# A two-layer hybrid decoder: seven block products for the output projection and most of the MLP's first matrix, with weight sums made by transfers

## The chip, the cores and the metric

The kernel runs on one core of a Trainium2 chip. The metric is the device time of one execution in microseconds; before the change it is 1337.68 us (median of three runs, 1336.81 to 1337.95). The engines are named as in the profile: PE is TensorE (PEld are its weight loads), DVE is VectorE, ACT is ScalarE, POOL is GpSimd, SP issues most transfers.

## What is computed

The reference is a decoder trunk with two layers over 512 tokens of width 1024, in float32. What matters here:

```python
def hybrid_layer(x, ...):
    h = rmsnorm(x, norm_mix)
    z = h @ w_in                                   # q, k, v | mLSTM q, k, v, o | gates
    ...                                            # att (512 wide), hm (512 wide)
    mixed = sigmoid(g_a) * (att @ w_att_branch) + sigmoid(g_m) * (hm @ w_m_branch)
    x = x + mixed @ w_out                          # 512x1024 @ 1024x1024
    u = relu(rmsnorm(x, norm_ffn) @ w_ff1)         # 512x1024 @ 1024x4096
    return x + (u * u) @ w_ff2                     # 512x4096 @ 4096x1024
```

`rmsnorm(x, g)` is `x * rsqrt(mean(x*x) + 1e-6) * g` with one factor per token.

## The kernel before

**Precision.** Each float32 operand of a large product is split into a high and a low piece of type float32r: ScalarE copies to the high one, VectorE subtracts it from the value to make the low one. `mm3` (line 207) then issues three matmuls into one PSUM bank, high x high, high x low, low x high. Weights come from HBM through SP's queue into raw tiles and are split on the way (`chunk`, line 164, in the mixer; `w_split`, line 820, in the MLP). Matmuls have a stationary operand of 128x128 and mostly 512 moving columns.

**Order of work.** Programs for the engines are written out as lists of steps. `weave` (line 251) runs a list `fill`, whose entries have a width, and inserts the steps of `side` at the places given. A planner at build time then fixes each engine's order: an instruction may go ahead of others whose operands are not ready, and what stands under `tc.high_priority()` (loads, splits, reads out of PSUM) goes first. Each engine runs its own list in order. A pool with n buffers makes the n+1st tile wait until the first one's readers are done.

**The mixer** (line 359) makes the projections, attention and mLSTM. At its end `ev_m` (line 786) multiplies the second branch with its gate and adds the first one, and splits the result tile by tile (`mixed`, 8 pairs of tiles of 128 features x 512 tokens). The output projection (lines 795 to 803) is `tok_steps` over these eight: two halves of 512 columns, 8 x 4 x 3 matmuls each; `ev_x` adds the result to the residual `xtok`.

**The norm** (`Norm`, line 275): `turn(k)` transposes 128 columns of the residual with four PE transposes, multiplies by the gain and splits (the tiles `i`); `squares` sums squares on ScalarE. The factor of the token isn't applied to the activations. In the MLP it was made with `columns` (one factor for each token), spread along the free axis with `along` (a diagonal, a float32 matmul with ones and a copy, line 310), and multiplied in `evac` (line 876), which reads a slot out of PSUM on VectorE: `max(ps, 0) * row`, then a square on ScalarE.

**The MLP** (line 806) goes through the 4096 hidden columns in four parts of 1024. A *first slot* (`First`, line 855) makes 256 hidden columns: 8 blocks of the contraction x 2 x 3 = 48 matmuls with the weights stationary and 512 tokens moving. The second matrix of a part (`slots_of`, line 921) is a 1024x1024 block with 512 tokens; it is computed as 2x2 blocks in seven products instead of eight (a Winograd form of Strassen's scheme). A product is 24 matmuls: left operand `a` of 256 tokens x 512 stationary, right operand of 512 x 512 moving. The sums and differences of weight blocks (`w_minus`) and of activation blocks (`u_op`) are made on VectorE; `gain` (line 845) adds a PSUM pair to the residual. While the second matrix of one part runs, the first slots of the next part stand between its products: p1, f, p5, p6, f, p3, p7, f, p2, f, p4. `prepare` (line 1011) writes the loads and splits of weights five half slots ahead.

## Time and profile before

| | before |
|---|---|
| median of the runs shown | 1337.68 us |
| span of the profiled execution | 1335.6 us |
| its own time (the span and some 2.1 us around it, taken from the median) | 1337.7 us |
| PE busy | 1312.4 us, 98% |
| DVE busy | 926.3 us, 69% |
| ACT busy | 666.4 us, 50% |
| POOL busy | 106.7 us, 8% |
| transfers | 125.02 MB, 30% of 16 engines' span |

A line of the profile's groups reads: source line, engine, operation, tile written <- tiles read, sizes, count | busy us, mean ns of one | idle time of the engine before them and what ended it. A line of the timeline reads: start, duration, engine, line, operation and tiles, count. Matmuls overlap, so the mean of one (about 390 ns) is a latency; the distance of starts is the price.

### The profile page before, as it was taken

What the parts mean: (1) busy time and instruction counts of PE and PEld (TensorE: products, weight loads), DVE (VectorE), ACT (ScalarE), POOL (GpSimd) and SP (SyncE); (2) the same over time, 40 slices, a digit from 0 to 9 for tenths busy, and PEclk for the clock granted to TensorE, in tenths of its full rate; (3) what the DMA queues carried; (4) which work ended last, traced back from release to release, by engine and by line L of the source; (5) the groups of instructions that cost most, each with busy time, mean ns of one, the idle gap of its engine ahead of it and who ended that gap; (6) DMA issues with size and microseconds to landing.
All of it is one profiled execution on the core that took longest, in us unless ns stands there. A gap on an engine that the chain in (4) does not pass through costs nothing.

```text
span 1335.6 us, 16885 instructions
## 1 busy us (share of the span) xinstructions
PE 1312.4 (98%) x6106; PEld 1078.1 (81%) x6106; DVE 926.3 (69%) x1409; ACT 666.4 (50%) x1201; POOL 106.7 (8%) x215
## 2 busy tenths in 40 slices
PE   8999999999999999999999999999999999999998
PEld 6877788888788888888888777888887888888886
DVE  4688764474576876868947887554646778678687
ACT  5458765544334344343554687554434444344343
POOL 4512310000000000000015013000000000000000
PEclk9999999999999999999999999999999999999999
DMA  5322122421523133131024221243216242322211
GB/s 151 108 72 72 56 79 74 140 95 64 189 95 126 63 127 125 64 119 46 34 65 123 67 71 64 72 122 96 99 54 207 73 132 81 125 95 95 95 48 63
DMA packets 87282, 125.02 MB, mean 94 GB/s; under 512 B 8216, under 2 KB 45184, under 8 KB 87200
## 3 DMA queue, kind: packets, MB, share of 16 engines
q1 hardware_dynamic: 86240, 123.30, 29.3%
q8 instruction: 48, 0.79, 0.2%
q10 hardware_dynamic: 576, 0.53, 0.1%
q0 software_dynamic: 384, 0.13, 0.1%
q14 instruction: 34, 0.28, 0.1%
HBM read 121.84 MB, written 2.10 MB: 93 GB/s over the span
## 4 chain that ended last, share of the span: by engine, by line
PE 88%; DVE 6%; ACT 4%; issue 1%; DMA 1%; POOL 0%; ACTq 0%; SPq 0%; DVEq 0%; POOLq 0%
PE mm L45 82%; PE aux L45 4%; PE aux L49 2%; ACT t L574 1%; DVE wl L191 1%; ACT wh L190 1%; DVE t L561 1%; DVE t L611 0%; DMA w<-in_w_in_dram 0%; DVE t L201 0%; ACT wh L825 0%; DVE t L538 0%; ACT junk L287 0%; DVE t L579 0%; DMA grow<-in_norm_mix_dram 0%
## 5 line engine op out<-in xcount | busy, mean ns | idle before, releaser
L45 PE MATMUL mm<-i,wh 128*128 128x512 f32 x1664 | 522.6, 393 | 2.1 <-DVE a L661 1.2
L45 PEld LDWEIGHTS mm<-i,wh 128*128 128x128 f32 x1664 | 307.7, 188 | 65.8 <-DVE a L661 2.0
L45 PE MATMUL mm<-i,wl 128*128 128x512 f32 x832 | 324.8, 390 | 0.0
L191 DVE TENSOR_TENSOR wl<-w,wh 128x512 fp32r<-128x512 f32 (+1 forms) x208 | 140.4, 677 | 131.7 <-ACT wh L190 126.8
L190 ACT ACTIVATE wh<-w 128x512 fp32r<-128x512 f32 (+1 forms) x208 | 127.2, 612 | 146.9 <-PE mm L45 123.8
L825 ACT ACTIVATE wh<-raw 128x1024 fp32r<-128x1024 f32 x112 | 118.3, 1056 | 151.9 <-PE mm L45 116.4
L45 PEld LDWEIGHTS mm<-i,wl 128*128 128x128 f32 x832 | 156.2, 188 | 33.0 <-issue 0.5
L45 PE MATMUL mm<-wh,uh 128*128 128x512 f32 x448 | 174.5, 389 | 0.0
L45 PE MATMUL mm<-wh,ul 128*128 128x512 f32 x448 | 174.3, 389 | 0.0
L45 PE MATMUL mm<-wl,uh 128*128 128x512 f32 x448 | 174.3, 389 | 0.0
L826 DVE TENSOR_TENSOR wl<-raw,wh 128x1024 fp32r<-128x1024 f32 x112 | 135.9, 1219 | 37.8 <-ACT wh L825 37.4
L45 PE MATMUL mm<-wh,i 128*128 128x512 f32 (+1 forms) x512 | 149.8, 371 | 0.4 <-ACT wh L190 0.4
L825 ACT ACTIVATE wh<-f 128x1024 fp32r<-128x1024 f32 x64 | 67.2, 1056 | 118.8 <-PE mm L45 92.3
L45 PEld LDWEIGHTS mm<-wh,i 128*128 128x128 f32 x512 | 92.7, 189 | 15.9 <-ACT wh L190 0.8
L826 DVE TENSOR_TENSOR wl<-f,wh 128x1024 fp32r<-128x1024 f32 x64 | 77.7, 1221 | 30.3 <-ACT wh L825 30.1
L45 PEld LDWEIGHTS mm<-wh,ul 128*128 128x128 f32 x448 | 84.1, 188 | 17.5
L45 PEld LDWEIGHTS mm<-wh,uh 128*128 128x128 f32 x448 | 84.1, 188 | 17.4
L45 PEld LDWEIGHTS mm<-wl,uh 128*128 128x128 f32 x448 | 84.1, 188 | 17.3
L45 PE MATMUL mm<-wl,i 128*128 128x512 f32 (+1 forms) x256 | 94.7, 370 | 0.0
L879 DVE SCALAR_TENSOR_TENSOR u<-mm,t 128x1024 f32<-128x1024 f32 x32 | 39.1, 1222 | 69.2 <-PE mm L45 69.1
L849 DVE TENSOR_TENSOR x<-x,mm 128x1024 f32<-128x1024 f32 x64 | 77.2, 1217 | 13.6 <-PE mm L45 13.6
L45 PE MATMUL mm<-wh,a 128*128 128x512 f32 x256 | 81.4, 393 | 0.0
(214 smaller groups left out, 1619.0 us busy)
## 6 DMA issues: line engine op xcount, KB each, us to landing
w<-in_w_in_dram SPq DMA_DIRECT2D x128, 256.0 KB, 2.6
f<-in_w_ff_dram SPq DMA_DIRECT2D x64, 512.0 KB, 3.7
raw<-in_w_ff_dram SPq DMA_DIRECT2D x64, 512.0 KB, 3.5
w<-in_w_out_dram SPq DMA_DIRECT2D x32, 256.0 KB, 2.5
w<-in_w_att_branch_dram SPq DMA_DIRECT2D x16, 256.0 KB, 2.5
w<-in_w_m_branch_dram SPq DMA_DIRECT2D x16, 256.0 KB, 2.5
w<-in_w_in_dram SPq DMA_DIRECT2D x16, 128.0 KB, 2.1
out_dram<-x SPq DMA_DIRECT2D x8, 256.0 KB, 2.2
```

Source lines behind the costliest of these rows:

```text
L45: return nc.tensor.matmul(*args, **kw)
L49: return nc.tensor.transpose(*args)
L190: sc.activation(wh[:, :off], raw[:, :off], AF.Copy)
L191: ve.tensor_tensor(wl[:, :off], raw[:, :off], f32(wh[:, :off]), op=ALU.subtract)
L561: ve.copy_predicated(dst, tri_i.unsqueeze(1).to_broadcast([P, 2, P]), p4[:, :, 1, :])
L574: sc.activation(s3[:, i, :], s3[:, i, :], AF.Exp, bias=m[:, i:i + 1], accum_out=den[:, i:i + 1])
L825: sc.activation(hi, r, AF.Copy)
L826: ve.tensor_tensor(lo, r, f32(hi), op=ALU.subtract)
L849: ve.tensor_tensor(xh, xh, ps, op=ALU.add)
L879: ve.scalar_tensor_tensor(dst, self.ps, 0.0, rowf[0].unsqueeze(1).to_broadcast([P, 2, T]), op0=ALU.max, op1=ALU.mult)
```

## The change

1. **Output projection.** `mixer` returns the unsplit sum as two tiles of 4 x 128 features x 512 tokens (`mixed`); the add is done on POOL. `mlp` begins with the projection, as one `second(None, mixed)`: seven block products in the order 1, 2, 5, 6, 3, 7, 4, in halves.
2. **First matrix.** The first 512 hidden columns stay as two plain slots (`Plain`, which reads out with `Relu` and `Square` on ScalarE). Each further group of 512 columns (`first`, seven groups in a layer) is done as seven block products of 24 matmuls, with the weight blocks stationary (512 x 256) and the left blocks moving (256 tokens). The combinations of the normed activations are made once a layer (`left_blocks`: 4 sums of high and low, 4 differences, 4 splits). Results are gathered in the tile `u`: `copy` on ScalarE, `finish` as a sum on VectorE and `Relu` and `Square` on ScalarE. Two groups stand between the products of each of the parts 0 to 2, by (2, 3, 3, 2, 2, 2, 0) after p1, p5, p6, p3, p7, p2, p4; the group of part 0 stands alone before them.
3. **Weight sums.** Signs are moved to the left operands and the gains, so that the right operands are plain sums. They are built by accumulating transfers (`accum_op=ALU.add`) on POOL's queue (`Weights`): b12+b11, then +b22, then +b21 in one tile, b22+b12 in the other.
4. **Norm factor.** relu(r h)^2 = r^2 relu(h)^2, so the MLP leaves the factor out and `gain` multiplies each result of the second matrix by r^2 = 1/v of its token (`inverse`), two half-width operations in place of one.
5. **Buffers.** Raw weights 9, splits 4 (`SPL`), which is also how many units ahead weights are prepared. A pool `half` for the whole kernel holds the attention's result, `mixed` and the hidden columns of the parts 1 and 3. `sel` and `cm2` are made in each layer.

The diff, cut to its core:

```diff
-            self.acts[k] = split(ps, self.gain(k), get=lambda: inp.tile([P, T], F32R, tag="i", name=nm("i")))
+            if self.big is None:
+                self.big = [inp.tile([P, KT, T], F32R, tag=f"i{n}", name=nm("i")) for n in range(2)]
+            to = [t[:, k, :] for t in self.big]
+            self.acts[k] = split(ps, self.gain(k), get=lambda: to.pop(0))
...
+        def inverse(self):
+            v = sm([P, NB], "nv")
+            ve.tensor_tensor(v, self.ss[:, :, 0], self.ss[:, :, 1], op=ALU.add)
+            ve.tensor_scalar(v, v, 1.0 / D, EPS, op0=ALU.mult, op1=ALU.add)
+            self.inv = sm([P, 2, NB], "ninv", 2)
+            ve.reciprocal(self.inv[:, 0, :], v)
+            ve.tensor_scalar(self.inv[:, 1, :], self.inv[:, 0, :], -1.0, None, op0=ALU.mult)
...
                 ve.tensor_tensor(sgm[g][m], sgm[g][m], ps, op=ALU.mult)
-                ve.tensor_tensor(prod[i], prod[i], sgm[g][m], op=ALU.add)
-                mixed[i] = split(prod[i])
+                gp.tensor_tensor(mixed[g][:, m, :], prod[4 * g + m], sgm[g][m], op=ALU.add)
...
+            def load(self, name, h, i, j):
+                with tc.high_priority():
+                    self.t[name, h] = raw_tile(self.n)
+                    nc.sync.dma_start(self.t[name, h], self.src(h, i, j))
+            def add(self, name, h, i, j):
+                with tc.high_priority():
+                    nc.gpsimd.dma_start(self.t[name, h], self.src(h, i, j), accum_op=ALU.add)
+            def get(self, which, h):
+                t = self.t
+                if which == 1:
+                    self.load("11", h, 0, 0)
+                    self.load("sum", h, 0, 1)
+                    self.add("sum", h, 0, 0)
+                    return w_split(t["11", h])
+                if which == 2:
+                    self.load("21", h, 1, 0)
+                    return w_split(t["21", h])
+                if which == 3:
+                    self.load("22", h, 1, 1)
+                    r = w_split(t["22", h])
+                    self.add("22", h, 0, 1)
+                    return r
+                if which == 7:
+                    return w_split(t["22", h])
+                r = w_split(t["sum", h])
+                if which == 5:
+                    self.add("sum", h, 1, 1)
+                elif which == 6:
+                    self.add("sum", h, 1, 0)
+                return r
...
+                if scale:
+                    for i in range(2):
+                        b = 2 * t + i
+                        r2 = norm.inv[:, 0 if sign > 0 else 1, b:b + 1]
+                        ve.scalar_tensor_tensor(xh[:, i, :], ps[:, i, :], r2, xh[:, i, :], op0=ALU.mult, op1=ALU.add)
+                else:
+                    ve.tensor_tensor(xh, xh, ps, op=ALU.add if sign > 0 else ALU.subtract)
...
@@ left_blocks
+            with tc.high_priority():
+                r21, r22 = whole(1, 0), whole(1, 1)
+                minus(r22, r22, r21)
+                keep(5, r22)
+                r11 = whole(0, 0)
+                minus(r22, r22, r11, -1.0)
+                keep(6, r22)
+                r12 = whole(0, 1)
+                minus(r12, r22, r12, -1.0)
+                keep(3, r12)
+                minus(r21, r11, r21)
+                keep(7, r21)
...
@@ first, one product
+                    for m in range(2):
+                        c = slice(m * P, (m + 1) * P)
+                        for kt in range(4):
+                            mm3(ps[bank][:, H * m:H * (m + 1)], hi[:, kt, c], lo[:, kt, c], ah[:, kt, :], al[:, kt, :],
+                                fresh and m + kt == 0, False, skip_group_check=True)
...
+            return [slot(1, "a", True, (copy, 0, 0)), slot(5, "b", True, (copy, 1, 1)),
+                    slot(6, "a", False, (copy, 0, 1)), slot(3, "b", False, (finish, 0, 1)),
+                    slot(7, "a", False, (finish, 1, 1), (copy, 1, 0)),
+                    slot(2, "c", True, (finish, 0, 0)), slot(4, "d", True, (finish, 1, 0))]
...
+        run(second(None, mixed), norm.steps(1, 0.5, 0.5), 2)
+        us = [new_u(0)]
+        plain = [Plain(0, "f"), Plain(1, "x")]
...
+        left_blocks()
+        slots = first(0, 1, us[0])
         for part in range(4):
+            nxt = []
             if part < 3:
+                us.append(new_u(part + 1))
+                nxt = first(part + 1, 0, us[part + 1]) + first(part + 1, 1, us[part + 1])
+            for s, n in zip(second(part, us[part]), (2, 3, 3, 2, 2, 2, 0)):
+                slots += [s] + nxt[:n]
+                nxt = nxt[n:]
+        run(slots, nnorm.steps(1, 0.5, 0.5) if nnorm else [], 4)
```

360 lines of the change are left out of this document (186 added, 174 removed).

## The prediction

> **What bounds the kernel now.** I read the page first, then the waits of TensorE, then the stretches of the layer's second half, then the queue's own rows. Of the page, the span, the engines and the chain that ended last:
>
> ```profile
> span 1335.6 us, 16885 instructions
> PE 1312.4 (98%) x6106; PEld 1078.1 (81%) x6106; DVE 926.3 (69%) x1409; ACT 666.4 (50%) x1201; POOL 106.7 (8%) x215
> PE 88%; DVE 6%; ACT 4%; issue 1%; DMA 1%; POOL 0%; ACTq 0%; SPq 0%; DVEq 0%; POOLq 0%
> ```
>
> TensorE is busy for 98% and carries 88% of the chain. An average can hide stages, so the second half of layer 0 follows by stretches: the output projection, the first two 256-column slots of the MLP, the three parts in which products of the second matrix alternate with slots of the first, and the last part alone. The columns are length, then busy time and instructions of PE, PEld, DVE, ACT and POOL, clock, DMA share, GB/s.
>
> ```profile
> 293.60:340.50 46.90, 46.43 (x215) 38.11 (x213) 23.10 (x37) 18.69 (x32) 0.00 (x0) 1.00 0.20 65
> 340.50:363.00 22.50, 22.17 (x100) 17.71 (x101) 12.71 (x21) 10.12 (x19) 0.00 (x0) 1.00 0.82 272
> 376.20:619.50 243.30, 243.30 (x1075) 201.51 (x1074) 179.97 (x155) 102.51 (x99) 0.00 (x0) 1.00 0.30 98
> 619.50:660.00 40.50, 40.50 (x180) 33.55 (x179) 40.40 (x36) 20.59 (x20) 0.00 (x0) 1.00 0.13 46
> ```
>
> For 283.8 us on end PE has no idle time at all, at clock 1.00, while VectorE has 74% and the transfer engines 30% in the alternating parts. There a matmul removed is its whole pitch gained, as long as nothing else becomes late. VectorE is full in the last part (40.40 of 40.50) and still in time, since it splits weights ahead. "Busy" of PE counts overlapping matmuls once, so I take prices from the distance of starts: 15 triplets of 512 columns, and 19 triplets of the 264-column projection of keys, values and gates, each matmul with a weight load of its own.
>
> ```profile
> 379.63 0.62 PE L45 MATMUL mm<-i,wh 128*128 128x512 f32 x2
> 389.83 0.62 PE L45 MATMUL mm<-i,wh 128*128 128x512 f32 x2
> ...
> 40.02 0.40 PE L45 MATMUL mm<-wh,i 128*128 128x264 f32 x2
> 46.86 0.40 PE L45 MATMUL mm<-wh,i 128*128 128x264 f32 x2
> ```
>
> 512 columns: 10.20 us / 45 = 0.2267 us. 264 columns: 6.84 / 57 = 0.120 us.
>
> **The change, part by part: TensorE.** (a) The output projection goes from 192 matmuls a layer to 7 x 24 = 168, all of 512 columns: 2 layers x 24 x 0.2267 = 10.9 us less. (b) The first matrix had 16 slots x 48 = 768 matmuls a layer, 174.1 us. Now two plain slots stay (96 x 0.2267 = 21.8), and seven groups of 512 columns take seven products of 24 matmuls, 1176 in all, each with 256 moving columns. No long stream of exactly 256 columns is in the trace. Bounds: half the 512 price, 0.113, and the 264 price, 0.120. I take the near row scaled, 0.120 x 256/264 = 0.1164, since the overhead above the columns' share is in that row. Then 136.9 + 21.8 = 158.7, so 15.4 us less a layer, 30.9 in both (bounds 22.4 and 38.9). (c) The norm factor along the free axis is no longer spread over the partitions in the MLP:
>
> ```profile
> 358.94 0.39 PE L45 MATMUL mm<-i,wh 128*128 128x512 f32 x1
> 359.52 1.10 PE L45 MATMUL aux<-t,ones 128*128 128x512 f32 x2 [0.20 <-DVE t L315]
> 360.06 0.80 PE L45 MATMUL mm<-i,wh 128*128 128x512 f32 x1
> 360.69 0.40 PE L45 MATMUL mm<-i,wl 128*128 128x512 f32 x1
> ```
>
> From 358.94 to 360.69 stand 1.75 us for two ordinary matmuls of 0.45: 1.3 us go, twice 2.6. Its replacement, five tiny operations for 1/v instead of the root, has no reader until the first gain of the second matrix, some 20 us of PE later: nothing. TensorE's sum: 10.9 + 30.9 + 2.6 = **44.4 us less**.
>
> **What the other engines get.** The prices:
>
> ```profile
> L826 DVE TENSOR_TENSOR wl<-raw,wh 128x1024 fp32r<-128x1024 f32 x112 | 135.9, 1219 | 37.8 <-ACT wh L825 37.4
> L825 ACT ACTIVATE wh<-raw 128x1024 fp32r<-128x1024 f32 x112 | 118.3, 1056 | 151.9 <-PE mm L45 116.4 <-issue 20.9 <-ACT wh L825 9.9
> L849 DVE TENSOR_TENSOR x<-x,mm 128x1024 f32<-128x1024 f32 x64 | 77.2, 1217 | 13.6 <-PE mm L45 13.6
> L831 DVE TENSOR_TENSOR raw<-raw,raw 128x1024 f32<-128x1024 f32 x64 | 76.9, 1222 | 1.2
> L204 DVE SCALAR_TENSOR_TENSOR i<-aux,gcol,i 128x512 fp32r<-128x512 f32 x32 | 23.6, 747 | 12.2 <-ACT i L203 12.2
> L661 DVE TENSOR_TENSOR a<-mm,t 128x512 f32<-128x512 f32 x32 | 20.5, 681 | 2.7 <-PE mm L45 2.3
> L49 PE MATMUL aux<-ident,x 128*128 128x128 f32 x128 | 20.4, 284 | 0.7 <-DVE x L799 0.7
> L648 ACT ACTIVATE a<-a 128x512 f32<-128x512 f32 x32 | 18.7, 621 | 4.2 <-DVE a L661 4.1
> L466 POOL TENSOR_TENSOR t<-a 128x512 f32<-128x512 f32 x8 | 8.4, 1086 | 504.0 <-ACT a L378 504.0
> ```
>
> An alternating part needs on PE 336 x 0.1164 + 168 x 0.2267 = 77.2 us (360 x 0.2267 = 81.6 before). On VectorE: low halves of 28 weight pieces and 7 left operands and 4 differences, 39 x 1.22, plus 8 half-width sums and 16 half-width scaled gains at 0.681: 63.9 us; before 53 x 1.22 = 64.7. The eight weight differences that go pay for what comes. ScalarE: 35 x 1.056 + 24 x 0.621 = 51.9. Both fit, so I cost them at nothing there, with PE as the cover.
>
> The stretch before is tighter. In the projection VectorE now does 14 low halves, 4 differences, 7 left operands, 8 gains and 4 norm splits: 33 x 1.22 + 4 x 0.747 = 43.2 us, where the row above shows 23.10. In the plain slots and the lone first group it does 4 + 7 weight halves, 12 operations for the left blocks, 4 norm splits and 4 sums: 23 x 1.22 + 3.0 + 2.7 = 33.8. Together 77.0 us, against 38.1 + 21.8 + 19.6 of matmuls and 20.4 / 4 = 5.1 of one norm's transposes, 84.6, on PE. It fits only on average. The next product's left operand is a chain of difference, high half, low half (1.22 + 1.06 + 1.22 = 3.5 us) queued among weight pieces. Bounds: nothing if the splits run ahead, about 6 us a layer if half of the twelve left-block operations lie open; I take 3, so **+6**.
>
> At the projection's start the sums of both branches go to POOL at 1.086 each. The last of four ends about 3.3 us after the branch's last matmul, the left operand of the second product 2.28 later, 5.6, against 5.44 of PE in the first product; the pools of the new stage also open on memory that the mixer has just used, and the projection's loads (8 of 512 KB a layer on SP's queue, 16 of 256 KB before) wait for it. Zero to 2 us a layer; I take 1: **+2**. That POOL also sets the selector and the padded maxima once a layer delays nobody: it sat idle for hundreds of us there (L466's row).
>
> **The transfers.** 8 sums in the projection, 28 in the first matrix and 32 in the second now arrive as accumulating transfers of 512 KB on POOL's queue: 136 in all. No such transfer is in the trace. The nearest rows are plain loads of that size on SP's queue, small ones of both queues, and the time that POOL spends on issuing two with many pieces:
>
> ```profile
> raw<-in_w_ff_dram SPq DMA_DIRECT2D x64, 512.0 KB, 3.5
> w<-in_w_in_dram SPq DMA_DIRECT2D x16, 4.0 KB, 1.9
> grow<-in_m_head_norm_dram POOLq DMA_DIRECT2D x1, 4.0 KB, 2.0
> ```
>
> ```profile
> L130 POOL DMA_DIRECT2D cosx<-in_rope_cos_dram x1 | 1.0, 1011 | 0.0
> ...
> L138 POOL DMA_DIRECT2D gq<-in_att_q_norm_dram x1 | 0.7, 707 | 0.0
> ```
>
> A 4 KB transfer lands alike from both queues. At share 0.30 the engines moved 98 GB/s, so a full share is 327 GB/s and 512 KB hold all 16 engines for 1.6 us. Below, a sum costs a load, 3.5 us; above, three passes after one another (source, old contents, result) with a dear issue, 1.0 + 3.5 + 3.2 = 7.7. I take two passes: 0.7 to issue, 3.5, and 1.6 for the second: 5.8 us. A slot's weights are prepared four matmul units ahead of where the *next* slot uses them, 2 x 2.72 + 2 x 2.79 = 11.0 us. Where the second product of a first-matrix group follows the first at once, load, sum and split must fit in: 3.5 + 5.8 + 1.06 + 1.22 = 11.6, short by 0.6, at four places a layer: **+5**. Where a sum is added to a tile between two splits, 2.28 + 5.8 + 2.28 = 10.4 fits. A late sum holds ScalarE, whose queue runs in order; behind it stand the next pieces and the copies out of PSUM that PE waits for.
>
> Room in the engines: a part has 16 loads and 16 sums, 16 x 1.6 x (1 + 2) = 76.8 us at two passes, against 77.2 of PE. That just fits. The Trainium skill, page "Collectives: The Full Stack", section "The bandwidth ceiling: the fold count and why AG ≠ RS ≠ AR", says that an add inside a transfer halves the rate because it reads two sources on one ring. No run here shows it yet; by it an alternating part would stand at the limit of its transfers, which is the third case below.
>
> **The sum.** 44.4 less, 6 + 2 + 5 = 13 more: 31.4 us less. The profiled execution's span is 1335.6; the median of the runs shown, 1337.68, lies 2.1 above it for what is outside the span. 1337.7 - 31.4 = **1306.3 us**.
>
> **The rivals.** *All is hidden.* In the trace PE waits for nothing in 283.8 us, though VectorE was full in the last 40.5; if the new work is placed as well, 1337.7 - 44.4 = 1293.3, with half-price matmuls 1285. Against it: 77.0 of 84.6 us.
> *Transfers become the bound*: slower. Place: the six alternating parts. Price: 25.6 us of plain load and 25.6 k of sums a part, k passes. Over 77.2 the part lasts as long as its transfers; the gain of 44.4 / 6 = 7.4 us a part is gone at (77.2 + 7.4 - 25.6) / 25.6, k = 2.3. At k = 3, 102.4 us a part: 1293 + 6 x 25.2 = 1444. For it: 0.82 of the share was already used in the 22 us of prefetch above, and k of 2 leaves nothing for queueing. Against it: reads of two memories may overlap, and then k is under 2.
> *VectorE and late sums eat the gain*: the first stretch loses 6 a layer, each of some 20 adjacent places 1.6: 1337, no change.
> *The narrow products cost a weight load*: the mean of a LDWEIGHTS in the profile is 188 ns.
>
> ```profile
> L45 PEld LDWEIGHTS mm<-i,wh 128*128 128x128 f32 x1664 | 307.7, 188 | 65.8 <-DVE a L661 2.0 <-issue 1.4 <-DVE u L879 0.9
> ```
>
> If 188 ns bound the pitch, 2352 of them would take 442 us where 304.7 are taken now, and the time would be 1337.7 + 137.5 - 13.5 = 1462. The 264-column stream, a load for each and 0.120 apart, speaks against it.
>
> **How the numbers follow.** Forecast with small waits 0.57 (its own range 1297 to 1325); all hidden 0.19; transfers the bound 0.17; gain eaten 0.04; weight loads 0.03. A measurement of this kernel can tell about 0.2%, 2.7 us, from no change. Faster by more 0.76, within 0.04, slower 0.20. The range begins under the hidden case at 1287 and goes to 1345, the near edge of the transfers' case; it leaves out the half-price end and what lies above k = 2.3.
>
> **What would show it.** Right: about 2350 matmuls of 256 columns some 0.116 apart, 5.44 us from product to product in the projection, about 77 us from part to part, no idle time of PE in the alternating parts, sums that land in about 6 us, and PE's few waits at the lone first group. Wrong: a DMA share near 1.0 in these parts with ScalarE waiting for sums (transfers the bound); PE waiting for left operands while VectorE is at 95% or more around the plain slots (gain eaten); starts 0.15 us or more apart without any wait (weight loads).

## The result, and the profile after

The changed kernel takes 1514.6 us (median, 1509.1 to 1517.5) against 1337.8 us: 1.132 times the time before, 95% interval 1.130 to 1.134. Forecast were 1306, in a range of 1287 to 1345. One execution each of r3_half and r8_sinks below ran in a second, slower state at a lower granted clock (1845.3 us at 0.65, 1505.4 at 0.83), and no reading rests on them. The page of after, the lines that answer to those of before:

```profile
span 1512.7 us, 19434 instructions
PE 1348.8 (89%) x7062; PEld 1138.2 (75%) x7062; DVE 964.0 (64%) x1473; ACT 790.8 (52%) x1383; POOL 301.9 (20%) x371
PE 45%; DMA 22%; DVE 14%; issue 12%; ACT 5%; POOL 2%; POOLq 0%; DVEq 0%; ACTq 0%; SPq 0%
```

PE carried 88% of the chain that ended last; now it carries 45%, and transfers, 1% before, carry 22%. PE's busy time has grown, by 36 us, although its work is less: part of the time it runs at a lower clock (granted 0.95 in the mean, 1.00 before). The three alternating parts of layer 0 (length, busy time and instructions of PE, PEld, DVE, ACT, POOL, then clock, DMA share, GB/s):

```profile
418.70:514.50 95.80, 84.54 (x506) 75.24 (x505) 63.14 (x64) 49.91 (x62) 19.91 (x16) 0.95 0.82 169
514.50:613.80 99.30, 85.12 (x505) 75.37 (x504) 61.57 (x64) 48.75 (x59) 19.92 (x16) 0.93 0.81 170
613.80:714.50 100.70, 86.83 (x506) 77.04 (x506) 61.67 (x64) 48.81 (x60) 18.64 (x15) 0.92 0.74 154
```

A part takes 95.8 to 100.7 us where 81.6 were taken and 77.2 forecast. No engine is full: VectorE has 61 to 66%, the transfer engines a share of 0.74 to 0.82. So something waits in turn. The queues' rows and the waits of PE, ScalarE and POOL (us in total, times, longest):

```profile
q0 software_dynamic: 51712, 71.44, 29.2%
q1 hardware_dynamic: 85984, 123.30, 27.3%
...
raw<-in_w_ff_dram SPq DMA_DIRECT2D x128, 512.0 KB, 4.9
raw<-in_w_ff_dram POOLq DMA_DIRECT2D x120, 512.0 KB, 6.7
```

```profile
PE mm L47 <- ACT wh L832: 88.3, 27, 8.9
PE mm L47 <- DVE wl L833: 26.2, 25, 1.8
PE mm L47 <- ACT u L1028: 20.9, 15, 3.6
```

```profile
ACT wh L832 <- DMA raw<-in_w_ff_dram: 175.0, 38, 11.0
```

```profile
POOL raw L877 <- DVE wl L833: 477.8, 88, 25.8
```

Read from below: POOL may issue a sum into a tile only when VectorE has read the tile for the low half of the product before (88 times). ScalarE then waits for that sum, up to 11 us (in the trace all 38 of these waits end with a transfer that POOL issued), and behind it in its queue stand the next pieces and the copies out of PSUM. PE waits for ScalarE's high halves, 27 times, up to 8.9 us. Whether this is the *order* (waiting in turn) or the *rate* of the transfers is what the experiments have to tell.

The second loss stands at the start of the projection, on PE:

```profile
292.98 0.39 PE L47 MATMUL mm<-a,wl 128*128 128x512 f32 x1
300.82 0.79 PE L47 MATMUL mm<-wh,uh 128*128 128x512 f32 x1 [7.45 <-ACT wh L832]
303.45 0.80 PE L47 MATMUL mm<-wl,uh 128*128 128x512 f32 x1 [1.84 <-DVE wl L833]
```

### The profile page after: what moved, and what is told of

Same layout as the page of the kernel before. It is cut to its first block, busy times and chain, and to the rows that moved or that the text cites. A ratio compares the mean times of both kernels' runs of the same rounds, so it can differ in the third digit from the quotient of the medians.

```text
span 1512.7 us, 19434 instructions
## 1 busy us (share of the span) xinstructions
PE 1348.8 (89%) x7062; PEld 1138.2 (75%) x7062; DVE 964.0 (64%) x1473; ACT 790.8 (52%) x1383; POOL 301.9 (20%) x371
## 4 chain that ended last, share of the span: by engine, by line
PE 45%; DMA 22%; DVE 14%; issue 12%; ACT 5%; POOL 2%; POOLq 0%; DVEq 0%; ACTq 0%; SPq 0%
PE mm L47 37%; DMA raw<-in_w_ff_dram 17%; PE aux L47 6%; DVE wl L833 5%; DMA raw<-in_w_out_dram 4%; ACT wh L832 3%; DVE x L912 2%; PE aux L51 2%; POOL raw L877 1%; DVE ul L833 1%; DVE wl L193 1%; ACT t L595 1%; DVE t L582 1%; DVE t L632 0%; DMA w<-in_w_in_dram 0%
## 5 line engine op out<-in xcount | busy, mean ns | idle before, releaser
L833 DVE TENSOR_TENSOR wl<-raw,wh 128x1024 fp32r<-128x1024 f32 x246 | 296.7, 1221 | 224.7 <-ACT wh L832 224.2
L832 ACT ACTIVATE wh<-raw 128x1024 fp32r<-128x1024 f32 x246 | 253.2, 1052 | 328.5 <-DMA raw<-in_w_ff_dram 175.0
L47 PE MATMUL mm<-i,wh 128*128 128x512 f32 (+1 forms) x1216 | 333.0, 360 | 17.4 <-ACT wh L832 16.8
L877 POOL DMA_DIRECT2D raw<-in_w_ff_dram x120 | 149.2, 1271 | 650.9 <-DVE wl L833 452.6
L47 PEld LDWEIGHTS mm<-i,wh 128*128 128x128 f32 x1216 | 216.2, 195 | 48.6 <-ACT wh L832 17.2
L47 PE MATMUL mm<-i,wl 128*128 128x512 f32 (+1 forms) x608 | 216.8, 357 | 0.0
L47 PE MATMUL mm<-hs,wh 128*128 128x256 f32 x672 | 144.9, 316 | 30.4 <-ACT u L1028 20.9
L47 PEld LDWEIGHTS mm<-hs,wh 128*128 128x128 f32 x672 | 124.4, 224 | 38.7 <-ACT u L1028 26.8
L47 PE MATMUL mm<-hs,wl 128*128 128x256 f32 x336 | 104.8, 312 | 0.9 <-DVE wl L833 0.9
L912 DVE SCALAR_TENSOR_TENSOR x<-mm,ninv,x 128x512 f32<-128x512 f32 x128 | 90.8, 745 | 19.3 <-PE mm L47 19.3
```

What stands on the lines that cost most here:

```text
L47: return nc.tensor.matmul(*args, **kw)
L832: sc.activation(hi, src, AF.Copy)
L833: ve.tensor_tensor(lo, src, f32(hi), op=ALU.subtract)
L877: nc.gpsimd.dma_start(self.t[name, h], self.src(h, i, j), accum_op=ALU.add)
L912: ve.scalar_tensor_tensor(xh[:, i, :], ps[:, i, :], r2, xh[:, i, :], op0=ALU.mult, op1=ALU.add)
```

## Experiments on the sums

**r1_no_sums** leaves out all 136 sums; nothing takes their place.

```diff
             def add(self, name, h, i, j):
-                with tc.high_priority():
-                    nc.gpsimd.dma_start(self.t[name, h], self.src(h, i, j), accum_op=ALU.add)
+                pass
```

> Leaves out all 136 accumulating transfers (the tiles hold the first summand alone), keeps everything else of the change. Theory A (the sums made by transfers are what is late): the forecast without its sum term, 1295 to 1310 us, PE without idle time in the alternating parts, clock 0.99 or more. Theory B (the left blocks, the narrow products or VectorE's load are what costs): over 1450 us, with the same waits of PE as in the changed kernel.

Measured: 1349.7 us, 1.009 [1.007, 1.012]. The sums cost 165 us. But without them the kernel is still 12 us above before, not 36 below it: there is a second loss. Of the 165 us some 111 lie in the six alternating parts, 45 between the projection's start and part 0, and 10 in the last parts (from the starts of their matmuls in both traces). Two parts without sums:

```profile
395.00:475.10 80.10, 79.43 (x505) 71.32 (x505) 63.58 (x65) 51.04 (x63) 0.00 (x0) 1.00 0.36 110
475.10:555.20 80.10, 79.43 (x506) 71.53 (x505) 61.89 (x64) 49.11 (x59) 0.00 (x0) 1.00 0.35 105
```

**r2_plain** issues the same transfers without the add (`accum_op` dropped, so a tile holds its last block alone).

> Each accumulating transfer becomes a plain one of the same bytes into the same tile on the same POOL queue (the sum is lost, each tile holds the last piece loaded). Theory A1 (adding inside the transfer costs: engine time and landing nearly double): 1310 to 1370 us, landing from POOL near 4.5 us in place of 6.7. Theory A2 (the chain of load, second transfer and split, and POOL's own issue, are what costs, whatever the transfer does): 1450 to 1515 us.

Measured: 1412.9 us, 1.057 [1.054, 1.060]. The second transfer into a tile costs 63 us, the add in it another 102. Parts last 85 to 89 us. The time lies between the ranges of the two theories.

**r3_half** adds only half of each tile (the slice `0:n//2`, so half of each sum is left out).

> Each accumulating transfer adds only half of its tile (half the bytes and half the pieces; the other half is left unsummed), chain and issue count unchanged. If the bytes count (transfer engines at 81% of the alternating parts): about half of the 220 us between this kernel and one without sums goes, 1370 to 1420 us or less. If the fixed latency of each link counts: over 1450 us.

Measured: 1422.2 us (one run). With half the bytes 72 of the 165 us stay, 44%: the loss goes with the size of a sum.

**r4_micro** measures the transfers alone, no matmul: six in a row, each behind the one before, and 24 side by side on four tiles, first in pieces of 2 KB, then of 1 KB; plain from SP, plain from POOL, accumulating from POOL.

> A small program apart: chains of six 512 KB transfers one after another and 24 in four chains side by side, as plain loads from SP, plain loads from POOL and accumulating ones from POOL, for pieces of 2 KB and of 1 KB. Its output is not the reference's. Throughput theory: side by side, an accumulating one costs 1.8 to 2 times the engine time of a plain one (3.0 us against 1.6). Latency theory: alone it already lands 2 us or more later than a plain one from SP (3.5 us), and side by side it costs less than 1.5 times.

Worked out of its trace's issues and landings, us for 512 KB:

```
                 alone, issue to landing   24 side by side, each
2 KB  SP, plain          3.8                     1.66
      POOL, plain        4.3                     1.74
      POOL, add          6.1                     2.76
1 KB  SP, plain          3.7                     1.62
      POOL, plain        4.1                     1.72
      POOL, add          6.0                     2.83
```

An accumulating transfer alone lands in 6.1 us, 5.8 were assumed. Side by side it takes 1.7 times as long as a plain one; two passes were assumed. By these rates the 16 loads and 16 sums of a part need 16 x (1.66 + 2.76) = 70.7 us, less than a part lasts in any run. So the forecast had the price of a sum nearly right, and still missed by 160 us.

**r8_sinks** issues every sum from the same place in the program with its bytes, but into two tiles that nothing reads.

```diff
+        sink = [sk.tile([P, 4 * H], F32, tag=f"k{i}", name=nm("k")) for i in range(2)]
...
-                    nc.gpsimd.dma_start(self.t[name, h], self.src(h, i, j), accum_op=ALU.add)
+                    sink.append(sink.pop(0))
+                    nc.gpsimd.dma_start(sink[0].rearrange("p (n f) -> p n f", n=self.n), self.src(h, i, j), accum_op=ALU.add)
```

> All 136 accumulating transfers are issued at the same places with the same bytes, but into two tiles that nothing reads, so no split waits for a sum and no sum waits for a split (the weight sums are left out of the result; two of the nine raw tiles give their memory). Theory, waiting in a chain: load, sum and split stand one behind the other, and ScalarE's queue with them, while the transfer engines themselves have room (0.81 of the share at 100 us a part): near the kernel without sums, 1350 to 1380 us. Rival, the rate of the transfer engines: all loads and sums together need about 100 us a part, whoever waits: 1480 to 1515. In between, the part of the loss that remains is the engines' share, plain loads landing later because of the sums included.

Measured: 1419.2 us, 1.061 [1.059, 1.062], which looks like the middle. The stretches tell more than the total. The parts of layer 0, and PE at the start of the projection:

```profile
431.00:511.00 80.00, 79.33 (x504) 71.23 (x504) 63.48 (x65) 50.84 (x63) 23.63 (x19) 1.00 1.08 228
511.00:591.10 80.10, 79.43 (x506) 71.54 (x505) 61.91 (x64) 49.09 (x60) 9.57 (x8) 1.00 0.75 178
```

```profile
335.98 0.80 PE L47 MATMUL mm<-wh,uh 128*128 128x512 f32 x1 [42.73 <-ACT wh L837]
```

With the transfer engines at a share of 1.08 the part is as long as without any sum, 80.0. The whole loss against r1_no_sums is one wait of 42.7 us a layer (7.45 without the edit; 2 x 35.3 = 70.6 of the 69.5 us), a fault of this edit. POOL's rows show it:

```profile
292.53 1.20 POOL L883 DMA_DIRECT2D k<-in_w_out_dram  x1 [2.22 <-DMA k<-in_w_out_dram]
293.28 1.75 POOL L809 TENSOR_TENSOR u<-a,a 128x512 f32<-128x512 f32 x1
...
331.39 1.20 POOL L883 DMA_DIRECT2D k<-in_w_ff_dram  x1 [1.45 <-DMA k<-in_w_ff_dram]
332.15 1.74 POOL L809 TENSOR_TENSOR u<-a,a 128x512 f32<-128x512 f32 x1
```

Sums that wait for no split run ahead. They stand in POOL's queue between the mixer's last adds (L809), and each waits for the sum before it in its sink. For the same reason 19 sums fall into the first part, 8 into the second and none into the third; it is the first part that tells. So there it is not the rate: where nobody waits for the sums, they cost the part nothing.

**r5_pool and r6_dve** make the same sums from four plain loads, by POOL (the diff) or by VectorE (`ve` in its place).

```diff
+            def fold(self, to, of, h):
+                with tc.high_priority():
+                    gp.tensor_tensor(self.t[to, h], self.t[to, h], self.t[of, h], op=ALU.add) 
...
+                if which == 1:
+                    self.load("a", h, 0, 0)
+                    self.load("b", h, 0, 1)
+                    r = w_split(t["a", h])
+                    self.fold("a", "b", h)
```

> The same weight sums, but none by a transfer: four plain loads on SP's queue and four sums on POOL for every seven products (b11+b12, +b22, +b21, and b12+b22), the same values in the same order. Theory, the sums as transfers are what went wrong: POOL added 128x512 in 1.46 us, so 128x1024 in about 2.9 and 16 of them hold POOL for 47 of some 80 us of a part, ahead of the splits by a slot: 1350 to 1362 us, near the kernel without sums (1349.7). Rival, POOL's sums slow VectorE's operations beside them (a low half of 1.22 us becomes 1.5 or more while POOL works): the part goes from 80 to 90 us and the time to about 1410. Second rival, a sum on any engine is late because of the order load, sum, split alone: over 1450.

> The same four loads and four sums, the sums on VectorE at 1.22 us. An alternating part then asks 63.9 + 16 x 1.22 = 83.4 us of VectorE where the parts without sums lasted 80.1, so VectorE is the bound there by 3.3 us: 6 x 3.3 = 20, and about 8 a layer in the projection and around the lone first group, where VectorE was already estimated at 77 of 85 us: 1349.7 + 36 = 1386. Rival, VectorE's time is not spent evenly and every sum pushes a left operand or a gain back, PE's clock falls after the waits: 1420 or more. If POOL's sums cost VectorE as much as they take themselves, this run is faster than the one with POOL's sums.

Measured: on POOL 1514.8 us (1.133 [1.131, 1.135]), no better than by transfers; on VectorE 1425.0 (1.066 [1.064, 1.067]), 39 above its theory, as its rival has it (1420 or more). The groups of r5_pool:

```profile
L877 POOL TENSOR_TENSOR raw<-raw,raw 128x1024 f32<-128x1024 f32 x136 | 398.3, 2936 | 467.7 <-DVE wl L833 338.8 <-DMA raw<-in_w_ff_dram 124.1 <-DVE ninv L312 2.5
...
L833 DVE TENSOR_TENSOR wl<-raw,wh 128x1024 fp32r<-128x1024 f32 x246 | 405.8, 1661 | 85.0 <-ACT wh L832 84.5
```

The low half of VectorE takes 1661 ns in the mean where it took 1221: POOL's 398 us of sums cost VectorE 177 us (964 to 1141 busy). That is the first rival's mechanism, but it gives 1410 us; the time is the second rival's (over 1450, the order alone), and ScalarE waits 124.6 us for POOL's sums. The run doesn't separate the two. In r6_dve the first two parts have 78.9 and 79.4 us of VectorE work and last 83.8 and 88.3.

**r10_order** keeps all transfers and changes who stands between whom: slots of the first matrix one by one between *half* products, and a group's products as 1, 5, 3, 6, 2, 7, 4.

```diff
-            for s, n in zip(second(part, us[part]), (2, 3, 3, 2, 2, 2, 0)):
+            for s, n in zip(second(part, us[part]), (1, 1, 1, 1, 1, 1, 2, 1, 1, 1, 2, 1, 0, 0)):
...
-                    slot(6, "a", False, (copy, 0, 1)), slot(3, "b", False, (finish, 0, 1)),
-                    slot(7, "a", False, (finish, 1, 1), (copy, 1, 0)),
-                    slot(2, "c", True, (finish, 0, 0)), slot(4, "d", True, (finish, 1, 0))]
+                    slot(3, "b", False), slot(6, "a", False, (copy, 0, 1), (finish, 0, 1, "b")),
+                    slot(2, "c", True, (finish, 0, 0)),
+                    slot(7, "a", False, (finish, 1, 1), (copy, 1, 0)), slot(4, "d", True, (finish, 1, 0))]
```

(`second` returns half products here, and a left operand is prepared two slots ahead.)

> The changed kernel (1514.6 us) with all its accumulating transfers, in another order of work: the slots of the first matrix stand one by one between half products of the second matrix instead of in twos and threes between whole ones, and a group's products come as 1, 5, 3, 6, 2, 7, 4, so that a sum and the split that reads it are four units of some 2.75 us apart in place of one or two. Bytes, counts and prices are the same. Theory, the waits of the chain (split, sum of 6 to 7 us, split, in ScalarE's order): a sum then has 11 us where it needs about 6.5 + 2.3, so most of the 18 us that a part lost go: parts of 82 to 88 us, 1514.6 - 6 x 14 = 1430, down to 1400. The projection and the lone first group stay as they were. Rival, the rate at which transfers run beside each other sets the part: parts stay at 95 us or more, 1490 to 1515.

Measured: 1385.5 us, 1.036 [1.034, 1.037]: 129 us less than the changed kernel, 45 better than expected. Its parts and its transfers:

```profile
411.90:490.60 78.70, 78.70 (x506) 71.74 (x505) 63.72 (x65) 52.21 (x65) 19.95 (x16) 1.00 0.99 207
490.60:569.80 79.20, 78.93 (x505) 71.66 (x504) 61.91 (x64) 49.47 (x59) 19.96 (x16) 1.00 0.99 216
```

```profile
raw<-in_w_ff_dram SPq DMA_DIRECT2D x128, 512.0 KB, 5.8
raw<-in_w_ff_dram POOLq DMA_DIRECT2D x120, 512.0 KB, 7.9
```

A sum lands *later* than in the changed kernel (7.9 us for 6.7), the transfer engines are at 0.99, and PE is busy from end to end of the first part. What decides is how many slots lie between a sum and the split that reads it. That the left operands come two slots ahead is hardly the reason: in r1_no_sums they come one slot ahead, and its parts lasted 80.1. That settles it for the parts: the rate is no bound, the order is what costs. In the old order a longer transfer is a longer link of the chain, so r2_plain and r3_half gain as well. For the sums of the projection and of the lone group (the seven products ahead of part 0) these runs don't settle it.

## Experiments on the start and on the lone group

These ten runs are about the second loss: r1_no_sums lies 48 us above what the forecast leaves without its 5 us for sums, 1301. The first two leave the sums out, the others are built on r10_order.

**r7_early** (on r1_no_sums): three raw tiles on memory that the mixer still uses are passed over.

```diff
+        for _ in range(3):
+            gp.memset(raw_tile(4)[:, 0, 0:1], 0.0)
```

> The kernel without sums (1349.7 us; all 136 weight sums are left out), with one edit: the first three of the nine raw tiles of the stage, which lie over the mixer's last operands, are passed over on the first turn (a tiny memset on POOL takes them), so the projection's first loads go to memory that the mixer left long before. Theory, the 7.45 and 1.84 us for which PE waits at the start of the projection are the loads': both go, twice 9.3, and 2.2 us of half clock behind each: about 1327. Rival, PE then waits for the left operand (POOL's four adds, high and low half, about 5.7 us after the last branch matmul) instead: about 1340, PE's wait moved to ul. If the address is not what holds the loads, no change: 1349.

Measured: 1350.1 us, no change. The first load now lands at 280.0 instead of 297.6 (the third is still issued at 298.0), and PE waits the same 7.45 us. ScalarE's rows of the changed kernel say why:

```profile
287.48 1.06 ACT L832 ACTIVATE uh<-u 128x1024 fp32r<-128x1024 f32 x1 [4.50 <-POOL u L809]
298.76 1.06 ACT L832 ACTIVATE uh<-u 128x1024 fp32r<-128x1024 f32 x1 [10.22 <-POOL u L809]
299.73 1.04 ACT L832 ACTIVATE wh<-raw 128x1024 fp32r<-128x1024 f32 x1
```

The *second* left operand's high half, which needs POOL's adds of the second branch, was placed ahead of the first product's weights, and the queue runs in order.

**r9_start** (on r7_early) forces the first product's weights ahead, by one-column copies into the tiles that would come first.

```diff
+                for k, (hi, _) in enumerate(after):
+                    sc.activation(to[0][:, 0, k:k + 1], f32(hi[:, 0, 0:1]), AF.Copy)
```

> The kernel without sums and with the early loads (1350.1 us; all 136 weight sums are left out), with the order of the first splits of the projection forced: four one-column copies make the left operands of the second and third products (high half on ScalarE, difference on VectorE) wait for the first product's weight pieces. Theory, the waits of 7.45 and 1.84 us are ScalarE's and VectorE's in-order queues: the second left operand stood ahead of the first product's weights there and waited for POOL's adds; now the first product needs only the first branch's half, starts right behind the mixer, and hides POOL's adds; left over are about 2.3 us of high and low half of the second left operand: 2 x (9.3 + 2.2 - 2.3) = 18 less, 1332. Rival, the first product itself still waits, for its loads or its own left operand: at most half of it goes, 1341 or more.

Measured: 1349.5 us, again nothing. The first matmul came 6 us earlier, at 293.98, and then PE waited 4.71, 1.97 and 0.60 us: for VectorE, whose operations POOL's four adds made longer, and for the third load, again on memory in use. The theories of r7_early and r9_start both fell, and the rival of r9_start held in its time (1341 or more): one wait took the other's place.

```profile
295.11 1.79 DVE L836 TENSOR_TENSOR ul<-u,uh 128x1024 fp32r<-128x1024 f32 x1
296.83 2.28 DVE L836 TENSOR_TENSOR wl<-raw,wh 128x1024 fp32r<-128x1024 f32 x1
```

**r11_start** and **r12_plain4** (on r10_order). The first puts the adds of the second branch on VectorE and holds three raw tiles until the first weights are written; the second also does the lone group as two more plain slots. In r12_plain4 these slots read one block of the activations after the seventh left block had been written over it, so that part of its product is another one.

```diff
+                (ve if g else gp).tensor_tensor(mixed[g][:, m, :], prod[4 * g + m], sgm[g][m], op=ALU.add)
...
+        plain = [Plain(2, "f"), Plain(3, "y")]
...
-        slots = first(0, 1, us[0])
+        slots = []
```

> The kernel with the new order (1385.5 us, all sums by transfers), with the start of the projection changed: three raw tiles on memory that the mixer still uses are held back until the first weights are written, the first product's weight pieces stand ahead of the second and third left operands on ScalarE and VectorE (four one-column copies), and the second branch's four adds are done on VectorE (0.69 each) in place of POOL (1.46), so that POOL's queue is free for the first sums. Theory, what was in the way at the start were the order of the queues and the third to eighth load (issued only at 300.3 in the run before): PE's gap falls from 7.45 + 1.84 to the time of two products with the gate, two adds and one low half behind the mixer's last matmul, 2 x 0.69 + 2 x 0.69 + 1.22 = 4.0 us, and the gaps of 1.85, 0.76, 0.81 and 0.76 further on in the projection go: 2 x (9.3 - 4.0 + 2 + 2.2 of half clock) = 19 less, 1366. Rival, the projection is bound by its own eight sums (chained 6 to 7 us each, two adjacent half products apart): it ends when they end, and the gap only moves to a later product: 1380 or more.

> The kernel of the run before, with the lone first group of each layer (seven block products ahead of part 0, beside nothing) done as two more plain slots: 192 matmuls of half the groups' saving are given up, 43.5 - 38.1 + ... in numbers two plain slots of 48 x 0.2267 = 21.8 us for seven products of 24 x 0.120 = 20.2, so 1.6 us more on PE a layer, and the left blocks get 21.8 us more before their first use. Theory, the lone group pays for the left blocks' chain on VectorE and for four chained sums with nothing between them: PE's gaps there, 1.1 + 1.1 + 1.4 + 7.8 us a layer, and some 4 us of half clock behind them go: 2 x (11.4 + 4 - 1.6) = 28 less than the run before, 1338. Rival, the 7.8 us belong to part 0's first weights (their sums queue behind the group's), and stay: 1355.

Measured: 1389.8 and 1389.6 us; both theories miss. In r11_start the first load was issued at 293.6 again: the pool gave it a tile in use. The time is in its rival's range (1380 or more), and gaps of 2.89 and 2.37 us appear further on in the projection, but with late loads the run doesn't test the theory. In r12_plain4 the lone group's wait only changed its name, to the overwritten block:

```profile
PE mm L47 <- ACT i L834: 15.7, 2, 7.8
```

**r13_best** and **r14_lone** mend both; r14_lone keeps the lone group. (A tile's first place is moved by the order of the mixer's pools, and one tile is passed over; the seventh sum has a tile of its own in the projection.)

```diff
-        pool(phase, "wraw", 3)
         pool(phase, "wsp", 4)
         pool(phase, "act", 24)
+        pool(phase, "wraw", 3)
...
                 minus(r21, r11, r21)
-                keep(7, r21)
+            return lambda: keep(7, r21)
```

(The last two lines are in r13_best alone.)

> The new order (1385.5 us, all sums by transfers), and at the start of each MLP: the mixer's raw weights lie at the place that the first raw tiles are taken from, the one tile on operands in use is passed over, so that the first product's loads are issued ahead of the mixer's last matmul; the first product's low halves and its left operand's are made on POOL (idle then) and the second branch's adds on VectorE, so that VectorE's queue does not hold the first product back; the second left operand stands behind the first product's weights on ScalarE; the projection's seventh sum has a tile of its own (two loads more a layer). And the lone first group is two plain slots, with the left block that lies on the activations written only after them. Theory, all of PE's gaps between the mixer's end and part 0 are loads, sums and splits that queue behind one another: start 9.3 to about 2.5 us (two POOL operations of 2.9 against the mixer's last matmul), the 4.2 us inside the projection gone, the lone group's 11.4 and some 4 us of half clock gone for 1.6 us of PE: 1385.5 - 2 x (6.8 + 2 + 4.2 + 13.8) = 1332, the first version with this change that is not slower than the kernel before. Rival, the left blocks on VectorE (some 13 us a layer) hold the plain slots' splits and the gap stays at another place: 1350 to 1365.

> The same with the lone first group left as seven block products. Theory: only the start and the projection gain, 2 x (6.8 + 2 + 4.2) = 26 less than 1385.5, 1360, and PE's gaps in the lone group (1.1, 1.1, 1.4, 7.8) stay. If the lone group's gaps came from the late start (loads and sums of the projection still under way), they shrink with it: 1340 or less, and two more plain slots are not worth it.

Measured: 1352.9 us (1.011 [1.010, 1.013]) and 1376.4 (1.029 [1.028, 1.031]). The lone group costs 23.5 us: seven products with chained sums and nothing between them. Its wait in r14_lone is in the row

```profile
PE aux L47 <- ACT wh L838: 16.1, 2, 8.6
```

The start gave back 9 of the 26 us expected. r13_best lies in its rival's range (1350 to 1365), but not for the rival's reason: PE's gaps there are 1.93 and 3.76 us at the start and 5.07 inside the projection, and 0.5 in the plain slots.

**r15_all** and **r16_p3** (on r13_best): all eight adds on VectorE, and the projection's seventh sum one product later; r15_all also puts product 2 between 5 and 6 in the last part and gives the seventh sum its own tile there. In r15_all the next layer's norm reads half of the residual before product 7 is added to it.

```diff
-            return sum([p1, p2, p5, p6, p3, p7, p4] if out_ else [p1, p5, p6, p3, p7, p2, p4], [])
+            return sum([p1, p2, p5, p6, p3, p7, p4] if out_ else [p1, p5, p2, p6, p3, p7, p4] if end else [p1, p5, p6, p3, p7, p2, p4], [])
```

> The version with the plain slots (1352.9 us), with all eight adds of the two branches on VectorE (0.69 us each, in the 7.6 us in which it stood idle before the mixer's last matmul and behind it) and the first product's low halves still on POOL, now before and not beside the adds; the seventh sum's own tile is loaded one product later in the projection, and in the last part too, where product 2 stands between 5 and 6. Theory, what was left at the start are operations of POOL and VectorE that slow each other (an add of 0.69 us took 2.82 there, a difference of 1.22 took 4.10) and the sums that compete with the seventh's: PE's 1.93 + 3.76 us fall to 1 or less, the 5.07 us inside the projection to about 2, the last part from 42 to 46 us to 40: 1352.9 - 2 x (4.7 + 2 + 3 + 3) = 1328, and the kernel before is beaten by some 10 us. Rival, the sums' chain in the projection stays what bounds it (5 to 6 us of gap at another product) and only the start gains: 1342.

> The same without the change of the last part (its order 1, 5, 6, 3, 7, 2, 4, the seventh sum in place). Theory: the last part's chained sums cost 3 us a layer, so 6 us more than the run with it, 1334. If the last part is bound by something else (VectorE was busy for 40.4 of its 40.5 us in the kernel before), the two runs are equal within 2 us.

Measured: 1346.1 and 1353.7 us. The times miss both theories (1328 and 1334) and the rival (1342); the difference is near the 6 us expected. The last part's chain is worth 7.6 us in the total: the last parts take 40.3 and 38.2 us for 46.9 and 41.7. r17_final, in which the norm doesn't read early, has 39.1 and 38.2, so that isn't the norm's doing (the mixer after it takes 4 us more). The start is unchanged, 1.9 + 3.8 us: the first left operand's tile now lay on weight pieces that PE read to the end, so POOL worked beside VectorE once more. Two adds took 4.40 us where the two before took 1.28:

```profile
292.69 1.28 DVE L809 TENSOR_TENSOR u<-a,a 128x512 f32<-128x512 f32 x2
293.89 1.27 DVE L808 TENSOR_TENSOR a<-a,mm 128x512 f32<-128x512 f32 x2
295.09 4.40 DVE L809 TENSOR_TENSOR u<-a,a 128x512 f32<-128x512 f32 x2
```

**r17_final** moves that tile back, passes three tiles over one by one, issues the projection's seventh sum one more product later, and weaves the norm into the last product alone (`run(..., 2)` for 4).

> The version of the two runs before with its two faults mended: the first product's left operand lies again on memory that the mixer leaves early (in those runs it lay on the mixer's weight pieces, which PE read to the end, so its high half waited until PE had finished), three raw tiles on operands in use are passed over one by one where the first product's loads would take them, and the next layer's norm is woven only into the last product, since product 7 now stands later in the last part. The seventh sum's load and sum are issued one product later. Theory, PE's 1.92 + 3.77 us at the start fall to 1 or less, now that both low halves can be made before the mixer's last matmul; with 2 us of half clock and some of the 5.18 us inside the projection, 1346.1 - 2 x (4.7 + 2 + 2) = 1329. Rival, the projection's own chain of sums (11 to 12 us each while the plain slots' loads and the seventh sums run beside them) sets its end whenever it starts: the gap of 5.18 grows by what the start gains, 1342 to 1346.

Measured: 1354.1 us, 1.012 [1.011, 1.014]. The theory misses, and the time lies above the rival's range (1342 to 1346). The first matmul follows the mixer at once, but then PE waits 4.99 and 1.63 us (the left operand's low half still waited for PE's last matmul), so the start gained nothing. The gap of 5.18 us inside the projection grew to 9.82, before product 6, for whose sum ScalarE waited 11.74:

```profile
327.33 1.06 ACT L838 ACTIVATE wh<-raw 128x1024 fp32r<-128x1024 f32 x1 [11.74 <-DMA raw<-in_w_out_dram]
```

Beside it run the loads of the plain slots and the seventh sums, and from 310 to 325 us the transfer engines stand at a share of 1.06 to 1.13. Here order and rate aren't separated.

**r18_plain_out** takes the sums out of the projection: eight block products in place of seven, each weight block loaded once and split for both token halves.

```diff
-        run(second(None, mixed), norm.steps(1, 0.5, 0.5), 2)
+        run(plain_out(mixed), norm.steps(1, 0.5, 0.5), 4)
...
+            for t, j, bank in ((0, 0, "x"), (0, 1, "f"), (1, 1, "y"), (1, 0, "x")):
+                for i in range(2):
+                    slots += product(t, j, i, bank)
```

> The version of the run before with the output projection as eight block products of 24 matmuls in place of seven: no sum and no difference of blocks there (8 loads a layer, each split twice, four left operands), 24 matmuls more a layer, 5.4 us; two plain pairs and the six groups beside the second matrix as before. Theory, the projection by seven products is bound by its chained sums (product 6 waited 9.8 us for a sum that landed 13 to 15 us after its issue, and POOL and VectorE lengthened each other at the start), so the stage from the projection's start to part 0 falls from 108 and 104 to 43.5 + 43.5 + 5 = 92, at most 97, and the start's 5 to 6 us stay: 1354.1 - (11 + 7) - some 6 of half clock = 1330, range 1324 to 1338: a version that beats the kernel before. Rival, what remains is VectorE's (16 low halves of weights, the norm's 8 splits and the adds between the mixer and the first plain slots) and not the sums': the stage stays at 100 or more and the time at 1345.

Measured: 1330.6 us, 0.9942 [0.9929, 0.9954]: 7.5 us faster than the kernel before, as expected. The stage from the projection to part 0 (first row) and two parts, and the page's chain:

```profile
292.70:388.20 95.50, 93.46 (x416) 76.21 (x417) 64.61 (x68) 49.52 (x64) 3.78 (x3) 0.98 0.48 133
388.20:466.80 78.60, 78.60 (x505) 71.80 (x504) 61.75 (x63) 51.53 (x61) 19.89 (x16) 1.00 1.00 208
466.80:546.20 79.40, 78.93 (x505) 71.73 (x505) 61.97 (x64) 49.48 (x60) 19.91 (x16) 1.00 0.98 212
```

```profile
span 1329.6 us, 19130 instructions
PE 1298.2 (98%) x6966; PEld 1104.4 (83%) x6966; DVE 939.6 (71%) x1461; ACT 782.5 (59%) x1361; POOL 253.8 (19%) x333
PE 83%; DVE 8%; DMA 4%; ACT 3%; issue 2%; POOL 0%; DVEq 0%; ACTq 0%; POOLq 0%
```

In r17_final the same stage took 108.1 us with 90.7 of PE work at clock 0.92. 24 matmuls more a layer, and 23.5 us less in both layers: in every order tried, the projection by seven products costs more in waits than it saves. Against its best stages (101.6 and 102.2 us, in r13_best) the plain one (95.5 and 93.6) still gains 14.7.

## Why the prediction was wrong

From 1306 to 1514.6 are 208 us.

- **The sums: forecast +5, measured +165.** The step that failed reads "A slot's weights are prepared four matmul units ahead ... 3.5 + 5.8 + 1.06 + 1.22 = 11.6, short by 0.6, at four places a layer". Its terms were somewhat small (a sum lands in 6.1 us alone, in 6.7 in the kernel; a load in 4.9 for 3.5), but that is the smaller part: with the kernel's landings the same working gives 13.9 for 11.6, short by 2.9 at eight places, 23 us. Wrong was to set each chain by itself against the whole lead. The prediction named the path ("A late sum holds ScalarE, whose queue runs in order"); its rival of the late sums priced it at 1.6 us in some 20 adjacent places, 32 us, with a chance of 0.04, and the loss was five times that. The lead of four units is one stock for all that ScalarE prepares. A split that waits for a sum holds ScalarE's queue, the splits behind it start late, and the next sum, which waits for such a split, is issued late. In a run of adjacent slots each sum needs 6.7 us to land and 2.3 for the split, 9 us, where the next slot is 2.8 us away. r10_order and the first part of r8_sinks show this: with more slots between, or with nobody waiting, the same transfers cost the parts nothing. For the 45 us between the projection's start and part 0 the same chain is likely, but no run shows it apart from the rate.
- **"Where a sum is added to a tile between two splits ... 10.4 fits"** failed in the same way: it fits once.
- **The rival "transfers become the bound"** had the right sign and the wrong mechanism. A k of 1.7 was below its point of 2.3, and at a share of 0.99 to 1.08 the parts lasted 78.6 to 80.3 us. Its sign, a share near 1.0 with ScalarE waiting for sums, came only in part: ScalarE waited, at a share of 0.74 to 0.82. The Trainium skill, "Collectives: The Full Stack", section "The bandwidth ceiling: the fold count and why AG ≠ RS ≠ AR", says of the reduce step of a ring collective that the two reads of its add halve the rate. For these loads into SBUF the add's rate is 0.60 of a plain load's (1.66 to 2.76 us), less than halved.
- **The narrow product: forecast 0.1164 us, measured 0.120**, from a stretch of r14_lone without waits; the second row is 20 matmuls after the first, 2.40 / 20:

```profile
382.48 0.40 PE L47 MATMUL mm<-hs,wh 128*128 128x256 f32 x2
384.88 0.28 PE L47 MATMUL mm<-hs,wl 128*128 128x256 f32 x1
```

  That is the upper end of the bounds, the price of 264 columns: 2352 x 0.0036 = 8.5 us of the gain.
- **The start: forecast 1 us a layer, measured 9.3**, 16.6 us too little in both. The step named POOL's adds and the memory, both rightly, but reckoned them against the second product. The planner had put the second left operand ahead of the first product's weights.
- **The rest, some 23 us**, is what else r1_no_sums loses. Its six parts last 80.1 to 80.3 us where 78.4 follow from the prices, some 11 us. Most of the other 12 lie between the projection and part 0: a lower clock behind the waits (0.94 there), the left blocks and the plain slots, where "I take 3, so +6" was too little. The runs don't separate these.
- **Right** were VectorE's load in the parts (63.9 forecast, 62 to 64 measured) and that PE would set their length once nothing waits (77.2 forecast, 78.4 by the measured price of the narrow product, 78.6 to 80.2 in layer 0 of r10_order and r18_plain_out).
- **A reading to set right:** the rows of before that the prediction calls parts are cut some 12 us early; the last part runs from 631.9 to 670.1. VectorE is busy for 37.90 of these 38.20 us, so what was read there holds.

What stays open: whether an order exists in which the projection by seven products pays. Of the edits of its start (r7_early to r17_final) the best gave back 9 us; with the others the wait moved elsewhere.

## What to carry to other kernels

A stock of prepared work covers one late operand, not a chain of them: where each link waits for the one before (split, sum, split) count the links per unit of the consumer's time, and put independent work between the links before counting bytes. Where an engine runs its queue in order, ask of every operand that is late *what stands behind it*. And read a run by its stretches before its total: the totals of r8_sinks, r12_plain4 and r17_final hid what their stretches showed.

## What the runs showed of the hardware

- An accumulating transfer of 512 KB lands in 6.1 us alone, plain ones in 3.8 (SP) and 4.3 (POOL); side by side 2.76, 1.66 and 1.74 (r4_micro). POOL spends 1.27 us to issue one in the changed kernel.
- At a DMA share of 0.99 and 1.00 PE was busy from end to end of a part (78.70 of 78.70 us in r10_order, 78.60 of 78.60 in r18_plain_out), at 1.08 for 79.3 of 80.0 (r8_sinks). In r10_order sums that land after 7.9 us were harmless to the parts.
- POOL and VectorE lengthen each other: in r5_pool a POOL sum took 2.34 us at least, 2.94 in the mean and 5.47 at most, and VectorE's low halves went from 1.22 to 1.66; at the start of r15_all a pair of adds of 1.28 us took 4.40.
- A matmul of 256 moving columns with a weight load of its own is 0.120 us from the next, no less than one of 264 columns (0.120).
